# Other scratch for one input product, and the bonus product of the second half beside the key norm's transposes

## The chip, the cores and the metric

The kernel runs on one core of one Trainium2 chip. The metric is the device time of one execution in microseconds (us). TensorE (PE in the profile) does the matmuls and the transposes, PEld is its weight load, DVE is VectorE, ACT is ScalarE, POOL is GpSimd, SP issues most of the weight transfers.

## The reference

One block in float32: a gated feed-forward network with half weight, a hybrid mixer, and a second feed-forward network, each between two root-mean-square norms, for 256 tokens of width 2048. The change lies in the mixer's recurrent branch (RWKV-7, width 1024, 16 heads of 64):

```python
r, k, v, lw, la, lg = jnp.split(zs, RWKV_SPLITS, axis=-1)      # zs = z + (shifted z - z) * mu
w = -jax.nn.softplus(-(w0 + jnp.tanh(lw) @ w2)) - 0.5
decay = jnp.exp(-jnp.exp(w))
a = jax.nn.sigmoid(a0 + la @ a2)
g = jax.nn.sigmoid(lg) @ g2
kk = k * k_k, divided by its norm in each head
k = k * (1.0 + (a - 1.0) * k_a)
y = _wkv7_scan(r_h, decay, k_h, v_h, -kk, kk * a_h)            # the recurrence over 256 tokens
y = group norm of y, * gn_w + gn_b
bonus = jnp.sum(r_h * k_h * r_k, axis=-1, keepdims=True) * v_h
y = (y + bonus) * g
```

r, k and v are columns of `p = u @ w_in`. The bonus needs r, the new k and v, and nothing of the recurrence.

## The kernel before, in words

All large products are made in three matmuls of 128x128 by 128x512 each, from operands split into a high and a low part (lines 367, 368 and 369). A weight tile of 128x1024 comes by a transfer on SP (line 329, buffers `w32`, four of them), is cast by ScalarE into its high part (line 343) and subtracted by VectorE into its low part (line 344); five buffers of each part stand between them and TensorE.

The mixer computes the recurrent branch in two halves of 512 columns (8 heads). For each half, three input products give k, v and r (`z_g`, through `across`). Such a product ends with these steps, which need three scratch tiles, here `sg`, `T1` and `x32`: ScalarE copies the result from PSUM to `sg` (line 1136), VectorE transposes blocks of 32 from `sg` to `T1` (line 1138), GpSimd issues 16 transfers from `T1` to `x32` (line 1147), and `shift` mixes each column with the one before, into the tile `zk`, `zv` or `zr` (ScalarE at line 1588, VectorE at line 1591).

`scratch` gives those three tiles. For products of the first half it hands out three of the 15 tiles R0 to R14 in turn; for the second half, three tiles of the pool `up`. That pool has `NUNITS = 33` places of 128x1024; a tile takes a place when it is first written and gives it back after its last reader. The 15 tiles R, the split input (8 tiles), results and `zk`, `zv`, `zr` all live in it.

`rwkv` is the recurrent branch of one half, written as a generator; the same R tiles serve both halves. Its steps in order, with their lines:

- kk = k * k_k (1845) to R3, its square (1846) to R5; small products pn (1852) for the head norms; pw and pa (1838, 1839) for decay and `a`; the sigmoids of the decay to R0 (1862) and of `a` to R2 (1869); running sums (1875) to R4; the exponentials `lam` to R0 (1879) and `ilam` to R1 (1880).
- transposes of v into the state (pV, 1905, copied out at 1910 and 1911).
- transposes of the norms (pk, 1919); kk times pk (1925).
- k2, the new k, to R5: ScalarE at 1927, VectorE at 1929, which is the last reader of `zk`; the products with `lam` and `ilam` (1930 to 1943), into R7 to R12.
- qb = r * r_k * k2 to R6 (1947), on VectorE.
- transposes and scores (pB 1963, pA 1976), with their masks (1985, 1987).
- the bonus: qb summed over each head by a product with a block of ones (pb, 2003), times v (2004).
- an inversion by substitution in 31 steps on VectorE (2020, 2022), and then the recurrence in four chunks.

Three things set the order of the work. TensorE's order is written by hand in the mixer (`manual_schedule`): `weave` runs `rwkv` to its next `yield x` and then puts x us of other products (`rest`: the remaining input products, the gates `gb_g`, `pb_g`) between. The order on the other engines is the planner's, which takes what is ready by priority, earlier program text first; weight casts and the ends of products have raised priority. PSUM has four banks (`pt`) for all the small products here and four for the large ones.

The first half's products, in order, are the low-rank inputs, two of the pooling branch, k, v and r. So they are the first to sixth call of `scratch`.

Of the kernel before, what the change touches and what calls it, by code (L numbers as in the profile page):

```python
# [12 lines left out]
AF = mybir.ActivationFunctionType  # L13
ALU = mybir.AluOpType
# [5 lines left out]
S = 256  # L20
# [241 lines left out]
class Block:  # L262
# [1330 lines left out]
    def mixer(s, prm, uT, rs, resid, emit, gpost, reload):  # L1593
# [49 lines left out]
        z = [{}, {}]  # L1643

        def z_g(hf, part=0):
            for nme, zc in ((("k", 1), ("v", 2), ("r", 0)), (("k", 1),),
                            (("v", 2), ("r", 0)), (("v", 2),), (("r", 0),))[part]:
                z[hf][nme] = s.unit((P, 4, S), F32, "z" + nme)
                c0 = zc * W + hf * 512
                yield from s.across(w_in, c0, at, rs, lambda v: s.shift(  # L1650
                    v, c0 // P, [z[hf][nme][:, i] for i in range(4)]), scratch(hf))
# [25 lines left out]
        turn = itertools.count()  # L1677

        def scratch(hf=0):
            n = next(turn)  # L1680
            if hf:
                return [s.unit(p="sc") for _ in range(3)]
            return [s.R[(3 * n + i) % 15] for i in range(3)]

        def pool_g(b):
            def done(v):
# [119 lines left out]
    def rwkv(s, hf, z, lz, prm, yH, yL):  # L1806
        nc = s.nc
        V, A, G, T = nc.vector, nc.scalar, nc.gpsimd, nc.tensor
        col = lambda nme, i: s.col[nme][:, hf * 4 + i:hf * 4 + i + 1]
# [4 lines left out]
        def reg(n, *shape):  # L1814
            t = s.R[n]
            if len(shape) == 2:
                return t.rearrange("p (a b) -> p a b", a=shape[0])
            if len(shape) == 3:
                return t.rearrange("p (a b c) -> p a b c", a=shape[0], b=shape[1])
            if len(shape) == 4:  # L1820
                return t.rearrange("p (a b c d) -> p a b c d", a=shape[0], b=shape[1],
                                   c=shape[2])
            return t
        ch = lambda t: t.rearrange("p i (c t) -> p i c t", c=NCH)
        fl = lambda t: t.rearrange("p i t -> p (i t)")
# [14 lines left out]
        k, v = z["k"], z["v"]  # L1840
# [17 lines left out]
        for q in range(2):  # L1858
            ps = s.psum("pw").rearrange("p (i t) -> p i t", i=2)
            lora(ps, 0, q)  # L1860
            for i in range(2):
                A.activation(out=sw[:, 2 * q + i], in_=ps[:, i], func=AF.Sigmoid,
                             bias=col("w0", 2 * q + i))
        a = reg(2, 4, S)
        for q in range(2):
            ps = s.psum("pa").rearrange("p (i t) -> p i t", i=2)
            lora(ps, 1, q)
            for i in range(2):
                A.activation(out=a[:, 2 * q + i], in_=ps[:, i], func=AF.Sigmoid,
                             bias=col("a0", 2 * q + i))  # L1870
# [29 lines left out]
        for pr in range(2):  # L1900
            pss = []
            for src in (v, vs):
                ps = s.psum("pV").rearrange("p (i c) -> p i c", i=4)
                for i in range(4):
                    T.transpose(ps[:, i], src[:, i, pr * P:pr * P + P], s.ident)
                pss.append(ps)
            for b in range(2):
                c = 2 * pr + b
                pe, po = pss[1 - b], pss[b]
                A.copy(EVs[O, :, c], pe[O, :, :64])  # L1910
                A.copy(ODs[E, :, c], po[E, :, 64:])
        yield 8.5
        pks = []
        for q in range(2):
# [3 lines left out]
                    o = h * 512 + (2 * q + i) * P  # L1918
                    T.transpose(ps[:, i, h * P:h * P + P], nbf[:, o:o + P], s.ident)
            pks.append(ps)  # L1920
        r = z["r"]
        k2 = reg(5, 4, S)
        for q in range(2):
            i2 = slice(2 * q, 2 * q + 2)
            V.tensor_tensor(out=kk[:, i2], in0=kk[:, i2], in1=pks[q], op=ALU.mult)
            for i in (2 * q, 2 * q + 1):
                A.activation(out=k2[:, i], in_=a[:, i], func=AF.Identity, scale=col("k_a", i),
                             bias=col("oka", i))
            V.tensor_tensor(out=fl(k2[:, i2]), in0=fl(k2[:, i2]), in1=fl(k[:, i2]), op=ALU.mult)
            V.tensor_tensor(out=fl(a[:, i2]), in0=fl(kk[:, i2]), in1=fl(a[:, i2]), op=ALU.mult)  # L1930
            for h, R in ((0, E), (1, O)):
                g8 = lambda t, sl: t[R, :, :, sl].rearrange("p i c t -> p (i c) t")
                V.tensor_tensor(out=g8(BK[q], h), in0=gr(a[R, i2]), in1=gr(ilam[R, i2]),
                                op=ALU.mult)
                V.tensor_tensor(out=g8(BK[q], 1 - h), in0=gr(k2[R, i2]), in1=gr(ilam[R, i2]),
                                op=ALU.mult)
                aa = g8(AR[q][h], 0)
                V.scalar_tensor_tensor(out=aa[:, :, 1:], in0=gr(kk[R, i2])[:, :, 1:],
                                       scalar=-1.0, in1=gr(lam[R, i2])[:, :, :C - 1],
                                       op0=ALU.mult, op1=ALU.mult)  # L1940
                V.tensor_scalar(out=aa[:, :, :1], in0=gr(kk[R, i2])[:, :, :1], scalar1=-1.0,
                                scalar2=None, op0=ALU.mult)
                V.tensor_tensor(out=g8(AR[q][h], 1), in0=gr(r[R, i2]), in1=gr(lam[R, i2]),
                                op=ALU.mult)
        qb = reg(6, 4, S)
        for i in range(4):
            V.scalar_tensor_tensor(out=qb[:, i], in0=r[:, i], scalar=col("r_k", i),
                                   in1=k2[:, i], op0=ALU.mult, op1=ALU.mult)
        lc = s.small(16, "lc", bufs=1)
        V.tensor_copy(lc, gr(lam)[:, :, C - 1])  # L1950
        lc4 = lc.rearrange("p (i c) -> p i c", i=4)
# [43 lines left out]
        yield 5.5  # L1995
        scores(1, 0)
        scores(1, 1)
        yield 6

        for q in range(2):  # L2000
            pb = s.psum("pb").rearrange("p (i t) -> p i t", i=2)
            for i in range(2):
                T.matmul(pb[:, i], s.bones, qb[:, 2 * q + i], start=True, stop=True)
            V.tensor_tensor(out=qb[:, 2 * q:2 * q + 2], in0=pb, in1=v[:, 2 * q:2 * q + 2],
                            op=ALU.mult)
        G.memset(EVs[E, :, 0], 0.0)
        G.memset(ODs[O, :, 0], 0.0)

# [8 lines left out]
        for kq in range(31):  # L2017
            n, m = kq // 2 + 1, 31 - kq
            pr = s.rtmp("pr")[:, :n * m].rearrange("p (a b) -> p a b", a=n)
            V.tensor_tensor(out=pr, in0=wt[:, kq + 1:, kq].unsqueeze(1).to_broadcast([P, n, m]),  # L2020
                            in1=tw[:, :n, kq:kq + 1].to_broadcast([P, n, m]), op=ALU.mult)
            V.tensor_tensor(out=tw[:, :n, kq + 1:], in0=tw[:, :n, kq + 1:], in1=pr,
                            op=ALU.add)
# [9 lines left out]
            A.copy(tt[R, :, o:o + 32], td[R])  # L2033
        for h in range(2):
            G.memset(tt[h * 64 + 32:h * 64 + 64, :, :32], 0.0)
        yield 44
        ps = s.psum("pM").rearrange("p (g t) -> p g t", g=16)
        for g in range(16):
            for h in range(2):
# [7 lines left out]
        for g in range(16):  # L2047
            for h in range(2):
                R = slice(h * 64 + 32, h * 64 + 64)
                T.matmul(ps[h * 64:h * 64 + 32, g], m1[R, g], tt[R, g, 32:64],  # L2050
                         start=True, stop=True)
# [13 lines left out]
        for c in range(NCH):  # L2065
            yield 1.8 if c else 0
            pu = v4(s.psum("pU"))
            for i in range(4):
                for R, h, ev in ((E, 0, EVs), (O, 1, ODs)):
                    T.matmul(pu[R, i], AR[i // 2][h][:, i % 2, c, 0], ev[:, i, c],  # L2070
                             start=True, stop=True)
# [14 lines left out]
            if c < NCH - 1:  # L2086
                pS = v4(s.psum("pS"))
                for i in range(4):
                    for R, h in ((E, 0), (O, 1)):
                        T.matmul(pS[R, i], BKt[i // 2][:, i % 2, c, h], ea_[:, h, i],  # L2090
                                 start=True, stop=True)
                st = s.rtmp("st").rearrange("p (i t) -> p i t", i=4)
                for R, ev in ((E, EVs), (O, ODs)):
                    V.tensor_tensor(out=st[R], in0=pS[R], in1=ev[R, :, c], op=ALU.add)
                    V.tensor_tensor(out=ev[R, :, c + 1], in0=st[R],
                                    in1=lc4[R, :, c:c + 1].to_broadcast([64, 4, C]),
                                    op=ALU.mult)
            py = v4(s.psum("pY"))
            for i in range(4):
                for R, h, ev in ((E, 0, EVs), (O, 1, ODs)):  # L2100
                    T.matmul(py[R, i], AR[i // 2][h][:, i % 2, c, 1], ev[:, i, c],
                             start=i == 0, stop=False, skip_group_check=True)
            for i in range(4):
                for R, h in ((E, 0), (O, 1)):
                    T.matmul(py[R, i], Xrb[R, i * NCH + c], ea_[R, h, i],  # L2105
                             start=False, stop=i == 3, skip_group_check=True)
# [5 lines left out]
                            op=ALU.subtract)  # L2112
# [5 lines left out]
                            op0=ALU.mult, op1=ALU.add)  # L2118
# [3 lines left out]
                            op=ALU.mult)  # L2122
# [11 lines left out]
        for q in range(2):  # L2134
# [7 lines left out]
            for i in range(2):  # L2142
                ii = 2 * q + i
                V.scalar_tensor_tensor(out=qb[:, ii], in0=pt[:, i], scalar=col("gn_w", ii),
                                       in1=qb[:, ii], op0=ALU.mult, op1=ALU.add)
                V.scalar_tensor_tensor(out=qb[:, ii], in0=qb[:, ii], scalar=col("gn_b", ii),
                                       in1=pg[:, i], op0=ALU.add, op1=ALU.mult)
            A.copy(yH[:, 2 * q:2 * q + 2], qb[:, 2 * q:2 * q + 2])
            V.tensor_tensor(out=yL[:, 2 * q:2 * q + 2], in0=qb[:, 2 * q:2 * q + 2],
                            in1=yH[:, 2 * q:2 * q + 2].bitcast(F32), op=ALU.subtract)  # L2150
# [108 lines left out]
```

## Time and profile before

| | |
|---|---|
| time, median of 3 runs (lowest to highest) | 2000.14 us (1999.96 to 2001.76) |
| the profiled execution | 2002.03 us |
| its span, first to last instruction | 2000.3 us |
| mean granted TensorE clock | 0.998 |
| busy: PE, DVE, ACT, POOL | 1987.1, 1812.9, 1223.4, 410.0 us |
| transferred | 472.37 MB, mean 236 GB/s |

The mixer with its recurrent branch lies between about 650 and 1330 us of the span. Times of instructions below are counted from the start of the span. In a list of instructions in order of time the columns are start, duration of the (possibly merged) row, engine, line, operation, tiles as out<-in, shapes, count, and in brackets the idle time of that engine just before and what ended it. A row for a stretch gives the busy time and the count of each engine, then the granted clock of TensorE, the share of the transfer engines, and GB/s.

### The profile page before, as it was taken

To read this page: it belongs to the slowest core of one execution; us is meant where nothing else is said; L and a number is where in the kernel's file an instruction comes from. 1 tells how busy PE (TensorE), PEld (TensorE's weight loads), DVE (VectorE), ACT (ScalarE), POOL (GpSimd) and SP (SyncE) were. 2 spreads that over 40 slices of the span, in tenths; PEclk is the share of its full clock that TensorE was granted. 3 is DMA by queue.
4 is the path that set the end of the run, shared out by engine and by line. 5 is a ranking of instruction groups with operands and counts; after the bars stand their busy time and mean duration, and the time that the engine had idled before them with its cause. 6 is when DMAs were issued, how large, how long until landed. Compare 5 with 4: busy or idle time off the path is not lost.

```text
span 2000.3 us, 29053 instructions
## 1 busy us (share of the span) xinstructions
PE 1987.1 (99%) x9903; PEld 1645.3 (82%) x9903; DVE 1812.9 (91%) x2467; ACT 1223.4 (61%) x1631; POOL 410.0 (20%) x747
## 2 busy tenths in 40 slices
PE   9999999999999999999999999999999999999998
PEld 7888888888888888888788888888888888888886
DVE  7999999999999957789789678989999999999997
ACT  7566665666666566675566434675666666666653
POOL 2000000574100113412320112010000115650000
PEclk9999999999999999999999999999999999999999
DMA  9868896987877777757556648869688889887774
GB/s 346 268 209 268 249 261 226 275 265 234 231 227 254 270 202 213 199 179 214 154 163 186 179 159 257 303 221 296 219 250 265 245 271 267 266 264 227 234 261 169
DMA packets 254086, 472.37 MB, mean 236 GB/s; under 512 B 27379, under 2 KB 31088, under 8 KB 253936
## 3 DMA queue, kind: packets, MB, share of 16 engines
q1 hardware_dynamic: 214128, 400.89, 61.0%
q0 software_dynamic: 39520, 69.08, 15.3%
q8 instruction: 78, 1.28, 0.3%
q14 instruction: 72, 0.59, 0.1%
q10 hardware_dynamic: 288, 0.52, 0.1%
HBM read 445.45 MB, written 8.39 MB: 227 GB/s over the span
## 4 chain that ended last, share of the span: by engine, by line
PE 97%; DVE 1%; issue 1%; ACT 1%; DMA 1%; SPq 0%; POOLq 0%; POOL 0%; DVEq 0%; ACTq 0%
PE mm L367 26%; PE mm L369 25%; PE mm L368 25%; PE ms L368 6%; PE ms L369 6%; PE ms L367 6%; PE tr L1015 1%; PE pA L1976 0%; DMA w<-in_w_in_dram 0%; DMA w<-in_ffn_gate_dram 0%; PE mc L977 0%; PE pU L2070 0%; PE pSa L2082 0%; PE pY L2105 0%; PE pT L2140 0%
## 5 line engine op out<-in xcount | busy, mean ns | idle before, releaser
L367 PE MATMUL mm<-wH,xH 128*128 128x512 f32 (+1 forms) x2008 | 783.2, 390 | 0.2 <-ACT xH L1024 0.2
L368 PE MATMUL mm<-wL,xH 128*128 128x512 f32 (+1 forms) x2008 | 779.3, 388 | 0.0
L369 PE MATMUL mm<-wH,xL 128*128 128x512 f32 (+1 forms) x2008 | 779.2, 388 | 0.1
L369 PEld LDWEIGHTS mm<-wH,xL 128*128 128x128 f32 x2008 | 377.2, 188 | 78.6 <-DVE xL L1033 1.1
L367 PEld LDWEIGHTS mm<-wH,xH 128*128 128x128 f32 x2008 | 377.1, 188 | 78.3 <-ACT xH L1024 0.5
L368 PEld LDWEIGHTS mm<-wL,xH 128*128 128x128 f32 x2008 | 377.2, 188 | 75.7 <-DVE wL L431 0.2
L677 ACT CAST wH<-t 128x1024 fp32r<-128x1024 f32 x244 | 256.8, 1054 | 209.5 <-DVE t L669 96.0
L421 ACT CAST wH<-w 128x1024 fp32r<-128x1024 f32 x293 | 301.6, 1052 | 118.7 <-PE mm L369 100.2
L431 DVE TENSOR_TENSOR wL<-w,wH 128x1024 fp32r<-128x1024 f32 x293 | 350.5, 1218 | 18.4 <-ACT wH L421 16.6
L343 ACT CAST wH<-w 128x1024 fp32r<-128x1024 f32 (+2 forms) x184 | 188.4, 1029 | 180.1 <-PE mm L369 155.4
L344 DVE TENSOR_TENSOR wL<-w,wH 128x1024 fp32r<-128x1024 f32 (+2 forms) x184 | 217.5, 1189 | 88.0 <-ACT wH L343 86.5
L682 DVE TENSOR_TENSOR wL<-t,wH 128x1024 fp32r<-128x1024 f32 x244 | 293.1, 1217 | 3.2 <-ACT wH L677 2.3
L677 ACT CAST wH<-w 128x1024 fp32r<-128x1024 f32 x244 | 199.6, 836 | 120.9 <-PE mm L369 91.0
L682 DVE TENSOR_TENSOR wL<-w,wH 128x1024 fp32r<-128x1024 f32 x244 | 229.1, 951 | 0.3
L1058 POOL DMA_DIRECT2D x<-T x352 | 179.0, 560 | 145.9 <-DVE wL L682 46.7
L655 POOL DMA_DIRECT2D t<-in_ffn_up_dram x47 | 57.4, 1227 | 567.3 <-DMA t<-in_ffn_up_dram 178.4
L368 PE MATMUL ms<-wL,sH 128*128 128x512 f32 x312 | 121.4, 389 | 0.0
L367 PE MATMUL ms<-wH,sH 128*128 128x512 f32 x312 | 121.4, 389 | 0.0
L369 PE MATMUL ms<-wH,sL 128*128 128x512 f32 x312 | 121.4, 389 | 0.0
L669 DVE TENSOR_TENSOR t<-w,t 128x512 f32<-128x512 f32 x122 | 83.4, 684 | 0.4 <-DMA w<-in_ffn_down_dram 0.2
L665 DVE TENSOR_TENSOR t<-w,t 128x512 f32<-128x512 f32 x122 | 82.9, 684 | 0.1
L660 DVE TENSOR_TENSOR t<-w,w 128x1024 f32<-128x1024 f32 x60 | 73.0, 1218 | 3.3 <-DMA w<-in_ffn_down_dram 3.3
(354 smaller groups left out, 2309.8 us busy)
## 6 DMA issues: line engine op xcount, KB each, us to landing
w<-in_w_in_dram SPq DMA_DIRECT2D x128, 512.0 KB, 4.4
w<-in_ffn_down_dram SPq DMA_DIRECT2D x104, 512.0 KB, 6.1
w<-in_ffn_up_dram SPq DMA_DIRECT2D x94, 512.0 KB, 5.7
w<-in_ffn_gate_dram SPq DMA_DIRECT2D x92, 512.0 KB, 6.9
w<-in_ffn_gate_dram SPq DMA_DIRECT2D x168, 256.0 KB, 5.8
w<-in_ffn_down_dram SPq DMA_DIRECT2D x131, 256.0 KB, 4.8
w<-in_ffn_up_dram SPq DMA_DIRECT2D x117, 256.0 KB, 5.9
t<-in_ffn_up_dram POOLq DMA_DIRECT2D x47, 512.0 KB, 7.7
```

The source lines that it names most:

```text
L343: s.nc.scalar.copy(vH, v)
L344: s.nc.vector.tensor_tensor(out=vL, in0=v, in1=vH.bitcast(F32), op=ALU.subtract)
L367: nc.tensor.matmul(ps, aH, bH, start=start, stop=False, skip_group_check=seeded)
L368: nc.tensor.matmul(ps, aH, bL, start=False, stop=False, skip_group_check=seeded)
L369: nc.tensor.matmul(ps, aL, bH, start=False, stop=stop, skip_group_check=seeded)
L421: nc.scalar.copy(x["H"], x["v"])
L431: nc.vector.tensor_tensor(out=x["L"], in0=x["v"], in1=x["H"].bitcast(F32), op=ALU.subtract)
L665: V.tensor_tensor(out=v["t24"][:, 0], in0=v["a"][:, 0], in1=v["t13"][:, 1], op=ALU.add)
L669: V.tensor_tensor(out=v["t24"][:, 1], in0=v["b"][:, 1], in1=v["t24"][:, 0], op=ALU.add)
L677: nc.scalar.copy(H, src)
L682: V.tensor_tensor(out=L, in0=src, in1=H.bitcast(F32), op=ALU.subtract)
L1058: nc.gpsimd.dma_start(out=x[0][q * 32:q * 32 + 32, i], in_=src[i * 32:i * 32 + 32, q])
```

## The change

`scratch` takes the start of the three R tiles from a list: the sixth call, r of the first half, now gets R6 to R8 instead of R0 to R2. The second half does not count its calls any more and takes tiles of the pool as before.

In `rwkv`, the work on k2, the weighing and the bonus become three local functions. In the first half they stand where they stood. In the second half, k2 (`extra`) and the weighing (`weigh`) stand ahead of the 8.5 us of filling before pk, and the bonus stands directly behind the transposes pk. The 6 us of filling that stood ahead of the bonus are added to the 44 us before the next product.

```diff
         def scratch(hf=0):
-            n = next(turn)
             if hf:
                 return [s.unit(p="sc") for _ in range(3)]
-            return [s.R[(3 * n + i) % 15] for i in range(3)]
+            n = (0, 3, 6, 9, 12, 6)[next(turn)]
+            return s.R[n:n + 3]
...
                 A.copy(ODs[E, :, c], po[E, :, 64:])
+        r = z["r"]
+        k2 = reg(5, 4, S)
+        qb = reg(6, 4, S)
+
+        def extra(q):
+            for i in (2 * q, 2 * q + 1):
+                A.activation(out=k2[:, i], in_=a[:, i], func=AF.Identity, scale=col("k_a", i),
+                             bias=col("oka", i))
+            V.tensor_tensor(out=fl(k2[:, 2 * q:2 * q + 2]), in0=fl(k2[:, 2 * q:2 * q + 2]), in1=fl(k[:, 2 * q:2 * q + 2]), op=ALU.mult)
+
+        def weigh():
+            for i in range(4):
+                V.scalar_tensor_tensor(out=qb[:, i], in0=r[:, i], scalar=col("r_k", i),
+                                       in1=k2[:, i], op0=ALU.mult, op1=ALU.mult)
+
+        def bonus():
+            for q in range(2):
+                pb = s.psum("pb").rearrange("p (i t) -> p i t", i=2)
+                for i in range(2):
+                    T.matmul(pb[:, i], s.bones, qb[:, 2 * q + i], start=True, stop=True)
+                V.tensor_tensor(out=qb[:, 2 * q:2 * q + 2], in0=pb, in1=v[:, 2 * q:2 * q + 2],
+                                op=ALU.mult)
+        if hf:
+            extra(0)
+            extra(1)
+            weigh()
         yield 8.5
         pks = []
...
-        r = z["r"]
-        k2 = reg(5, 4, S)
+        if hf:
+            bonus()
         for q in range(2):
             i2 = slice(2 * q, 2 * q + 2)
             V.tensor_tensor(out=kk[:, i2], in0=kk[:, i2], in1=pks[q], op=ALU.mult)
-            (k2 on ScalarE and VectorE)
+            if not hf:
+                extra(q)
...
-        (qb = r * r_k * k2)
+        if not hf:
+            weigh()
...
         scores(1, 1)
-        yield 6
-        (pb and its product with v)
+        if not hf:
+            yield 6
+
+        if not hf:
+            bonus()
...
-        yield 44
+        yield 50 if hf else 44
```

More of the change, by code (lines that the diff above doesn't have):

```diff
@@ L1925, in rwkv @@
             V.tensor_tensor(out=kk[:, i2], in0=kk[:, i2], in1=pks[q], op=ALU.mult)
[L1926 to L1929, printed above, removed]
+            if not hf:
+                extra(q)
             V.tensor_tensor(out=fl(a[:, i2]), in0=fl(kk[:, i2]), in1=fl(a[:, i2]), op=ALU.mult)
@@ L1944, in rwkv @@
                                 op=ALU.mult)
[L1945 to L1948, printed above, removed]
+        if not hf:
+            weigh()
         lc = s.small(16, "lc", bufs=1)
@@ L1997, in rwkv @@
         scores(1, 1)
-        yield 6
[L2000 to L2005, printed above, removed]
+        if not hf:
+            yield 6
+        if not hf:
+            bonus()
         G.memset(EVs[E, :, 0], 0.0)
```

## The prediction

> **What bounds the kernel now.** I read the totals and the chain of work first, then the busy time by stretches, then the orders of TensorE, ScalarE, VectorE and GpSimd around the two edits.
>
> ```profile
> span 2000.3 us, 29053 instructions
> PE 1987.1 (99%) x9903; PEld 1645.3 (82%) x9903; DVE 1812.9 (91%) x2467; ACT 1223.4 (61%) x1631; POOL 410.0 (20%) x747
> ...
> PE 97%; DVE 1%; issue 1%; ACT 1%; DMA 1%; SPq 0%; POOLq 0%; POOL 0%; DVEq 0%; ACTq 0%
> ```
>
> TensorE holds 97% of the chain. The order of its queue is written by hand, so what the change can give or take is time in which TensorE stands still; work on other engines is free as long as TensorE does not wait for it. The stretches of the mixer show where it stands:
>
> ```profile
> core 0: us, PE busy (x) PEld busy (x) DVE busy (x) ACT busy (x) POOL busy (x), PEclk, DMA share, GB/s
> 850.00:900.00 50.00, 48.48 (x285) 40.35 (x284) 43.68 (x74) 37.70 (x69) 8.02 (x9) 1.00 0.59 179
> 1000.00:1050.00 50.00, 50.00 (x337) 42.62 (x336) 41.65 (x76) 32.99 (x50) 12.91 (x20) 1.00 0.55 162
> ```
>
> The first half of the recurrence (around 850 us) loses 1.52 us; the start of the second half (1000 to 1050 us) loses nothing. So the first edit aims at a real hole, and the second touches a place that has none.
>
> **First edit: the scratch of r in the first half.** Before, r's product uses R0 to R2, and `a` (L1869) is written to R2, so `a` stands behind the last reading of r's scratch (L1588). `a` holds two of the four small PSUM banks meanwhile. TensorE and ScalarE there:
>
> ```profile
> 855.17 0.60 PE L1905 MATMUL pV<-ident,zv 128*128 128x128 f32 x4
> 855.61 0.60 PE L1905 MATMUL pV<-ident,R 128*128 128x128 f32 x4
> 857.73 0.66 PE L1905 MATMUL pV<-ident,zv 128*128 128x128 f32 x4 [1.52 <-ACT R L1910]
> 858.38 0.66 PE L1905 MATMUL pV<-ident,R 128*128 128x128 f32 x4
> 858.79 0.47 PE L367 MATMUL mm<-wH,xH 128*128 128x512 f32 x1
> ```
> ```profile
> 848.52 1.57 ACT L1862 ACTIVATE R<-pw,cols 128x256 f32<-128x256 f32 x4 [0.93 <-PE pw L1839]
> 864.25 0.91 ACT L1588 ACTIVATE zb<-R,cols 128x256 f32<-128x256 f32 x2
> 866.31 1.28 ACT L1869 ACT_TABLE_LOAD   x1
> 867.61 1.57 ACT L1869 ACTIVATE R<-pa,cols 128x256 f32<-128x256 f32 x4
> ```
>
> The four groups of pV want four banks. The banks of pn and pw are free (L1862 ended at 850.1), but both of pa are held until 869, so the third group waits until the first two are copied out. Four groups at 0.44 us (855.17 to 855.61) are 1.76 us; they took 855.17 to 858.79, 3.62. With R6 to R8 as scratch, `a` needs only pa and follows L1862 directly, until about 851.7, well ahead of 855. R6 to R8 become qb and BK later; their earlier user is a pool product two products back, so I price the new claim at nothing. Also gone is the table load at 866.31 (sigmoid before the exponential, not after): ScalarE time, off the path. Term: **-1.9 us** (bounds 0 and -1.9). What is late next is the weights: some casts already wait for their transfers a little later,
>
> ```profile
> 885.25 1.05 ACT L343 CAST wH<-w 128x1024 fp32r<-128x1024 f32 x1 [1.97 <-DMA w<-in_w_in_dram]
> 888.22 1.05 ACT L343 CAST wH<-w 128x1024 fp32r<-128x1024 f32 x1 [1.92 <-DMA w<-in_w_proj_b_dram]
> ```
>
> and a TensorE that arrives 1.9 us sooner could give some of it back there; but TensorE has no wait in that stretch now, and the work on ScalarE and VectorE that crowds 860 to 876 moves earlier too. I keep -1.9 and let 0 stand as the other end.
>
> **Second edit: the bonus beside pk.** Moved ahead of pk in the second half: four activations and two products (k2, `extra`), four weighings (`weigh`); moved from 6 us of filling after the scores to directly behind pk: four matmuls and two VectorE products (`bonus`). No DMA is issued by them, and the filling of TensorE is the same (44+6 became 50). What they cost themselves:
>
> ```profile
> 1038.33 1.04 PE L1919 MATMUL pk<-ident,R 128*128 128x128 f32 x8
> 1039.12 0.47 PE L367 MATMUL mm<-wH,xH 128*128 128x512 f32 x1
> ...
> 1082.51 1.89 PE L2003 MATMUL pb<-R,bones 128*128 128x256 f32 x8
> 1084.04 0.58 PE L367 MATMUL mm<-wH,xH 128*128 128x512 f32 x1
> ```
>
> pb takes 1.53 us (1082.51 to 1084.04) in either place. One change between small and large matmuls goes: a first L367 of 0.58 instead of 0.39, **-0.1 us** at most -0.2. Two VectorE products of 0.6 us leave the long series behind the scores, which hides them.
>
> The point is what pb waits for. `weigh` reads r, so pb now needs r of the second half when pk is done, at 1039.1. Before, when is that r ready?
>
> ```profile
> 976.31 0.69 ACT L1136 ACTIVATE sc<-mm,rs 128x512 f32<-128x512 f32 x1 [1.84 <-PE mm L369]
> ...
> 1031.92 0.69 DVE L1929 TENSOR_TENSOR R<-R,zk 128x512 f32<-128x512 f32 x1
> 1032.53 1.22 DVE L344 TENSOR_TENSOR wL<-w,wH 128x1024 fp32r<-128x1024 f32 x1
> 1033.66 1.30 DVE L1138 STREAM_TRANSPOSE sc<-sc 128x512 f32<-128x512 f32 x2
> ...
> 1062.47 0.48 DVE L1947 SCALAR_TENSOR_TENSOR R<-zr,cols,R 128x256 f32<-128x256 f32 x1
> ```
>
> r leaves PSUM at 977, but its transposes come only at 1033.66, and the last weighing ends at 1062.95. The code says why: `s.unit` has 33 places, claimed at the first write. At 977 there are live 15 R, 8 of the input, lq, 2 of the finished first yT, 4 yb, zk, zv and the copy just made: 33. The transposes need one more, and the next to fall free is zk, whose last reader is the second L1929. It is the instruction just before them but for one weight product. The change does not free a place: L1929 is in `extra`, behind the same `a`. After the transposes comes GpSimd:
>
> ```profile
> 1035.25 6.46 POOL L1147 DMA_DIRECT2D sc<-sc x13 [6.28 <-DVE sc L1138]
> 1042.45 0.98 POOL L1147 DMA_DIRECT2D sc<-sc x2 [0.74 <-DMA sc<-sc]
> 1044.09 0.50 POOL L1147 DMA_DIRECT2D sc<-sc x1 [0.66 <-DMA sc<-sc]
> DMA to landing us min/median/max: 2.5/4.5/6.4
> ```
>
> Sixteen copies fill every part of r's transposed form, so nothing of r can be shifted before the last has landed. It is issued at 1044.09; by 2.5 to 6.4 us it lands between 1046.6 and 1050.5. I take 3.5, between the least and the median, because GpSimd had waited for earlier copies to land and few are before it: 1047.6. Then the shift and the weighing:
>
> ```profile
> 1053.43 0.51 ACT L1588 ACTIVATE zb<-sc,cols 128x256 f32<-128x256 f32 x1
> 1053.84 0.50 ACT L1588 ACTIVATE zr<-sc,omu 128x256 f32<-128x256 f32 x1
> 1054.71 0.89 DVE L1591 TENSOR_TENSOR zr<-zr,zb 128x256 f32<-128x256 f32 x2
> ```
>
> Eight activations at 0.41 (1053.43 to 1053.84) are 3.3 us, one sum 0.45, one weighing 0.48: 4.2, with 0.1 for the hand-overs 4.3, so the last operand stands at 1051.9. ScalarE and VectorE are free for it, for with TensorE standing no weight buffer falls free and no cast is due. The last half of pb is 0.8 more: filling goes on at 1052.7. Without the wait it would at 1039.12 + 1.53 = 1040.65. Term: **+12.0 us** of standing TensorE, which nothing covers, since every matmul is queued behind pb.
>
> Bounds: at the short end L1929 comes as early as its input allows.
>
> ```profile
> 1024.88 1.14 ACT L1927 ACTIVATE R<-R,oka,cols 128x256 f32<-128x256 f32 x2
> ...
> 1030.17 1.09 ACT L1927 ACTIVATE R<-R,oka,cols 128x256 f32<-128x256 f32 x2
> ```
>
> If the second pair followed the first, before the exponentials, all behind it would be 4.1 us earlier (1030.17 to 1026.0), and with the least landing another 1.0: +6.9. At the long end the shift keeps its old date, last weighing 1062.95 plus 0.8: +23.1. I am nearest to the middle, because the exponentials stand ahead of k2 in the program in both kernels, and because the casts that delayed L1588 before are not there when TensorE stands.
>
> **The clock.** A standing TensorE also comes back slow. This run has one such place, its start, after an idle of 1.33 us:
>
> ```profile
> 6.86 0.66 PE L1015 MATMUL tr<-ident,x 128*128 128x128 f32 x4 [1.33 <-DMA x<-in_x_dram]
> ```
> ```profile
> 8.00:10.00 2.00, 1.74 (x4) 0.63 (x4) 1.90 (x7) 2.00 (x7) 1.58 (x4) 0.67 1.07 397
> 10.00:12.00 2.00, 2.00 (x8) 1.71 (x8) 1.56 (x4) 0.90 (x4) 0.41 (x1) 0.50 1.05 385
> 12.00:14.00 2.00, 2.00 (x10) 1.64 (x9) 1.50 (x5) 1.40 (x3) 0.00 (x0) 0.98 1.05 372
> ```
>
> Granted 0.67, 0.50 and 0.98: 0.66 + 1.00 + 0.04 = 1.7 us of clock lost. But the 1.52 us hole at 856 left the clock at 1.00, so idle does not always cost. For 11 us of idle I take the start's value: **+1.7 us** (bounds 0 and 1.7). The Trainium skill, page "TensorE: Matmul & The Clock Gate", Part 1, speaks against the change: after an idle window of about 3.4 us the clock drops to half and needs about 3.4 us of activity to return. By that page alone the hole at 856 is too short to count, as the trace has it, and the new one would cost an estimated 1.7 us; the start's drop after 1.33 us is not what its window leads one to expect.
>
> **Sum.** -1.9 - 0.1 + 12.0 + 1.7 = +11.7 us. The profiled execution took 2002.0 us with a span of 2000.3; it stands 1.9 above the median of 2000.14. A span of 2012.0, and against the median 2011.8, which I give as **2011.8**.
>
> **Rivals.** (1) Short wait: L1929 and the copies move up, +6.9 instead of +12.0, giving 2006.7, or 2005.0 without the clock's term. For it: VectorE no longer has L1935 ahead of the second L1929 in the program. Against: the exponentials come first, and GpSimd's sixteen issues keep their 9.3 us. (2) Long wait: shift late, +23.1, 2022.9; for it the old date of L1588, against it the empty ScalarE. (3) No wait, the other side: r's transposes get a place before the second half starts, so that r is weighed before pk is done. All r's steps from L1138 on take 1033.66 to 1051.9, 18.2 us, so this decides from a place free by 1020.9; then only -1.9 - 0.1 is left, 1998.1. Against it is the count of 33; for it, that 56 us pass between 977 and 1033 and one freed place would do. (4) The first edit brings nothing, because the weights are late at 885: 2013.7, inside the forecast's own range.
>
> **How the numbers follow.** Forecast with rival 4, 0.60, own range 2008 to 2016; short wait 0.20, 2003 to 2008; long wait 0.09, 2016 to 2023; no wait 0.11, around 1998. Leaving out most of no wait and the upper part of the long one gives 2003 to 2018. About 0.2% (4.0 us) is what a measurement of this kernel can tell from no change. No wait lies within that, save 0.03 for a larger gain in the first half; a tenth of the short waits ends below 2004.1: faster 0.03, same 0.10, slower 0.87.
>
> **What would show it.** First half: no idle before the third pV group, L1869 right behind L1862, and no table load before it. Second half: one idle of TensorE of some 9 to 12 us at pb, directly behind pk, released by VectorE's weighing (the first half of pb may run 2 us sooner); L1138 still right behind the second L1929; L1588 within a microsecond of the last landing; a granted clock near 0.5 for the 3 us after it. The prediction is wrong if r's transposes stand well ahead of 1033, if TensorE goes from pk to pb without a hole, or if the filling after it finds weights missing.

## The result, and the profile after

| | before | after |
|---|---|---|
| median (lowest to highest) | 2001.08 us (1999.96 to 2003.08), 5 runs | 2018.89 us (2016.32 to 2022.57), 5 runs |
| ratio after/before, 95% interval | | 1.009, 1.0079 to 1.0101 |
| the profiled execution, its span | 2002.03, 2000.3 us | 2016.32, 2014.6 us |
| mean granted clock of the profiled execution | 0.998 | 0.995 |

The change makes the kernel slower by 17.8 us. The forecast was 11.7; the median lies 0.9 us above the end of the range (2018.0). The profiled execution of the changed kernel is the fastest of its five, so the profile shows less than the medians do.

The page of the changed kernel, span, busy time and chain:

```profile
span 2014.6 us, 29018 instructions
...
PE 1988.2 (99%) x9903; PEld 1645.3 (82%) x9903; DVE 1814.0 (90%) x2467; ACT 1224.4 (61%) x1631; POOL 408.3 (20%) x747
...
PE 95%; DVE 2%; ACT 1%; issue 1%; DMA 1%; POOL 0%; POOLq 0%; DVEq 0%; SPq 0%; ACTq 0%
```

Hardly anybody's work grew (TensorE 1988.2 against 1987.1 us), yet the span did: TensorE stands still more. Its share of the chain fell from 97% to 95%, and VectorE's rose from 1% to 2%. The stretches of the changed kernel say where:

```profile
core 0: us, PE busy (x) PEld busy (x) DVE busy (x) ACT busy (x) POOL busy (x), PEclk, DMA share, GB/s
850.00:900.00 50.00, 48.10 (x284) 40.11 (x283) 42.76 (x68) 36.92 (x68) 6.10 (x8) 1.00 0.59 176
1000.00:1050.00 50.00, 39.12 (x272) 33.56 (x273) 40.87 (x78) 31.87 (x54) 12.92 (x20) 0.92 0.55 158
1050.00:1100.00 50.00, 48.11 (x274) 38.95 (x274) 31.94 (x46) 27.97 (x50) 2.68 (x5) 0.94 0.48 137
```

The stretch from 1000 us stood full before; now 10.9 us of it are empty. The first half (from 850 us) still loses 1.90 us, where it lost 1.52. TensorE's own rows, in order of time:

```profile
854.16 0.60 PE L1905 MATMUL pV<-ident,R 128*128 128x128 f32 x4
854.60 0.60 PE L1905 MATMUL pV<-ident,zv 128*128 128x128 f32 x4
...
878.60 0.50 PE L368 MATMUL mm<-wL,xH 128*128 128x512 f32 x1 [1.90 <-DVE wL L344]
...
1036.83 1.04 PE L1945 MATMUL pk<-ident,R 128*128 128x128 f32 x8
1048.75 2.05 PE L1931 MATMUL pb<-R,bones 128*128 128x256 f32 x4 [10.88 <-DVE R L1924]
1052.68 2.04 PE L1931 MATMUL pb<-R,bones 128*128 128x256 f32 x4 [1.89 <-DVE R L1924]
1054.17 0.99 PE L367 MATMUL mm<-wH,xH 128*128 128x512 f32 x1
```

The hole ahead of the third pV group is gone, and a new one of 1.90 us stands 24 us later, at a large product that waits for the low part of a weight. In the second half TensorE waits 10.88 and 1.89 us between pk and the end of pb.

Numbering the large products and setting the start of each beside that of the same product before gives the steps of the difference: -1.96 us at pV, +2.06 at 878.60, -0.29 near 965, +16.55 at the product behind pb (1039.12 before, 1054.17 here), +0.87 over the next three, -1.73 at 1084, where pb used to be. With the steps too small to list this is +15.7. The span differs by only 14.3, because the start-up of this execution was shorter: from 13 us on every product stands 1.41 us earlier than before. That has nothing to do with the change. The granted clock stayed at 1.00 from 8 to 14 us here, where it had fallen to 0.50 before.

ScalarE, VectorE and GpSimd of the changed kernel around both edits:

```profile
847.01 1.57 ACT L1862 ACTIVATE R<-pw,cols 128x256 f32<-128x256 f32 x4 [0.86 <-PE pw L1839]
848.46 0.86 ACT L1869 ACTIVATE R<-pa,cols 128x256 f32<-128x256 f32 x2
...
1046.71 0.51 ACT L1588 ACTIVATE zb<-sc,cols 128x256 f32<-128x256 f32 x1 [10.00 <-DMA sc<-sc]
```
```profile
1030.44 0.69 DVE L1920 TENSOR_TENSOR R<-R,zk 128x512 f32<-128x512 f32 x1
1031.04 1.22 DVE L344 TENSOR_TENSOR wL<-w,wH 128x1024 fp32r<-128x1024 f32 x1
1032.17 1.30 DVE L1138 STREAM_TRANSPOSE sc<-sc 128x512 f32<-128x512 f32 x2
...
1049.38 1.38 DVE L1967 TENSOR_TENSOR R<-zr,R 64x512 f32<-64x512 f32 x2
1050.79 0.76 DVE L1591 TENSOR_TENSOR zr<-zr,zb 128x256 f32<-128x256 f32 x2
1051.46 0.68 DVE L1932 TENSOR_TENSOR R<-pb,zv 128x512 f32<-128x512 f32 x1
1052.06 0.87 DVE L1924 SCALAR_TENSOR_TENSOR R<-zr,cols,R 128x256 f32<-128x256 f32 x2
```
```profile
1033.76 6.49 POOL L1147 DMA_DIRECT2D sc<-sc  x13 [6.29 <-DVE sc L1138]
...
1043.65 0.50 POOL L1147 DMA_DIRECT2D sc<-sc  x1 [1.62 <-DMA sc<-sc]
```

The chain of the stall is read from the bottom up: the last of r's sixteen copies is issued at 1043.65, the shift (L1588) starts at 1046.71 after ScalarE has stood for 10.00 us, and the last weighing ends at 1052.93. L1138, the first step of that chain, stands two instructions behind the second k2 product (L1920), the last reader of `zk`.

### The profile page after: what moved, and what is told of

The parts are those of the page before. It is cut to its first block, busy times and chain, and to the rows that moved or that the text cites. A ratio compares the mean times of both kernels' runs of the same rounds, so it can differ in the third digit from the quotient of the medians.

```text
span 2014.6 us, 29018 instructions
## 1 busy us (share of the span) xinstructions
PE 1988.2 (99%) x9903; PEld 1645.3 (82%) x9903; DVE 1814.0 (90%) x2467; ACT 1224.4 (61%) x1631; POOL 408.3 (20%) x747
## 4 chain that ended last, share of the span: by engine, by line
PE 95%; DVE 2%; ACT 1%; issue 1%; DMA 1%; POOL 0%; POOLq 0%; DVEq 0%; SPq 0%; ACTq 0%
PE mm L367 25%; PE mm L369 25%; PE mm L368 25%; PE ms L369 5%; PE ms L367 5%; PE ms L368 5%; PE tr L1015 1%; DMA sc<-sc 0%; PE pA L1998 0%; ACT wH L343 0%; DVE wL L344 0%; PE pU L2089 0%; PE pSa L2101 0%; DMA w<-in_ffn_gate_dram 0%; PE pY L2124 0%
```

## The experiments

The kernels ran in three groups, each beside 21 runs of the kernel before.

| kernel | median (lowest to highest), runs | ratio, 95% interval |
|---|---|---|
| before, first group | 2000.67 (1999.93 to 2002.91), 21 | |
| e1_scratch | 2002.98 (2001.11 to 2004.11), 11 | 1.0009, 1.0000 to 1.0018 |
| e2_bonus | 2016.60 (2015.70 to 2017.73), 4 | 1.008, 1.0066 to 1.0093 |
| e3_place | 2004.26 (2001.79 to 2005.06), 11 | 1.0016, 1.0007 to 1.0025 |
| e5_filled | 2017.92 (2015.04 to 2021.96), 4 | 1.0087, 1.0074 to 1.0101 |
| before, second group | 2000.63 (1999.54 to 2002.44), 21 | |
| e6_filled2 | 2016.73 (2014.86 to 2017.45), 5 | 1.0077, 1.0065 to 1.009 |
| e7_k2_early | 2000.25 (1999.74 to 2003.42), 11 | 1.0, 0.9991 to 1.0009 |
| e8_place_only | 2001.46 (2000.71 to 2002.25), 11 | 1.0002, 0.9994 to 1.0011 |
| e9_mix_apart | 2017.13 (2016.52 to 2018.93), 4 | 1.0082, 1.0069 to 1.0096 |
| before, third group | 2000.50 (1999.79 to 2003.01), 21 | |
| e10_weigh_late | 2003.65 (2001.78 to 2004.51), 11 | 1.0014, 1.0005 to 1.0023 |
| e13_late_alone | 2001.15 (2000.38 to 2001.78), 11 | 1.0, 0.9991 to 1.0009 |
| e12_weigh_first | 2018.78 (2017.31 to 2019.19), 5 | 1.0089, 1.0076 to 1.0103 |

**The two edits apart.** e1_scratch is the kernel before with the first edit alone:

```diff
         def scratch(hf=0):
-            n = next(turn)
             if hf:
                 return [s.unit(p="sc") for _ in range(3)]
-            return [s.R[(3 * n + i) % 15] for i in range(3)]
+            n = (0, 3, 6, 9, 12, 6)[next(turn)]
+            return s.R[n:n + 3]
```

> The first edit alone. Theory W (the 1.96 us that the third pV group no longer waits are given back 25 us later, where TensorE waits for a weight's low part behind VectorE's queue, 1.90 us in the changed kernel): the same time as before, within 0.5 us of it, no idle before the third pV group and one of 1.5 to 2 us at about 879 us. Rival F (the give-back comes from the second edit's new order on VectorE, not from the first edit): 1.9 us faster than before, no idle at 879.

Measured: 2.3 us above the kernel before, at the edge of what can be told from no change, and no gain; the idle ahead of the third pV group is gone and one of 1.90 us stands at 879, as expected. The time was expected within 0.5 us of before. TensorE and its stretches in e1_scratch:

```profile
879.66 0.50 PE L368 MATMUL mm<-wL,xH 128*128 128x512 f32 x1 [1.90 <-DVE wL L344]
```
```profile
880.00:882.00 2.00, 2.00 (x8) 1.58 (x7) 2.00 (x4) 0.87 (x2) 0.00 (x0) 0.67 0.61 143
882.00:884.00 2.00, 2.00 (x6) 1.62 (x5) 1.97 (x4) 0.75 (x1) 0.00 (x0) 0.50 0.80 224
884.00:886.00 2.00, 2.00 (x10) 1.55 (x10) 1.97 (x4) 0.72 (x2) 0.00 (x0) 0.97 0.83 246
```

The 1.96 us won at pV are lost again 23 us later in one wait of 1.90 us. In this execution the granted clock falls behind that wait to 0.67, 0.50 and 0.97: 0.66 + 1.00 + 0.06 = 1.7 us, most of the 2.3 by which the medians differ. In the profiled execution of the changed kernel the same wait left the clock at 1.00.

Which weight product is late shows when casts and low parts are counted, in order of time. ScalarE's casts and VectorE's low parts in e1_scratch, then the same two rows in the kernel before:

```profile
870.59 1.05 ACT L343 CAST wH<-w 128x1024 fp32r<-128x1024 f32 x1
```
```profile
866.59 1.22 DVE L344 TENSOR_TENSOR wL<-w,wH 128x1024 fp32r<-128x1024 f32 x1
...
872.03 1.21 DVE L344 TENSOR_TENSOR wL<-w,wH 128x1024 fp32r<-128x1024 f32 x1
...
878.39 1.22 DVE L344 TENSOR_TENSOR wL<-w,wH 128x1024 fp32r<-128x1024 f32 x1
```
```profile
873.11 2.00 ACT L343 CAST wH<-w 128x1024 fp32r<-128x1024 f32 x2
```
```profile
867.08 1.23 DVE L344 TENSOR_TENSOR wL<-w,wH 128x1024 fp32r<-128x1024 f32 x1
...
870.20 1.21 DVE L344 TENSOR_TENSOR wL<-w,wH 128x1024 fp32r<-128x1024 f32 x1
...
876.90 1.22 DVE L344 TENSOR_TENSOR wL<-w,wH 128x1024 fp32r<-128x1024 f32 x1
```

In e1_scratch the third wide cast behind 865 us ends at 871.6, but its low part stands on VectorE only at 878.39; before, the same cast ended at 874.1 and its low part started at 876.90. So the cast came 2.5 us sooner and its low part 1.5 us later: VectorE's order now has more of the recurrent products ahead of it, which the earlier `a` had made ready. The delay arises one low part earlier: from the first to the second row of e1_scratch 5.44 us pass, before only 3.12, because two products of k2 and `ilam` (L1935), two sums of r's shift (L1591) and one weighing (L1947) now stand in between. There was little room for it. Before, this low part ended at 878.12 and TensorE used it at 879.94, so its slack was 1.8 us.

e2_bonus is the second edit alone (the diff of the change without the hunk above).

> The second edit alone. Theory R (TensorE stands at pb until r of the second half is weighed, and the clock comes back late): 17 to 18 us slower than before, all of what the whole change costs, with the idle of 1.5 us at the third pV group back and no idle at 879. Rival S (the two edits act on each other, so that the first one's new order makes r later in the second half): less than 14 us slower.

Measured: +15.9 us on the median, and by its trace a step of 15.88 us at the product behind pb, with another 2.0 us at half clock right behind it. There is no idle at 879. It was expected to cost 17 to 18 us, and one sign failed: the idle of 1.52 us at the third pV group did not come back whole, but is 0.40 us. It is as short in the other kernels without the first edit (0.66 in e7_k2_early, 0.49 in e8_place_only, 0.40 in e13_late_alone), with ScalarE in the same order there. In the profile of the kernel before, two of ScalarE's casts ahead of pV's copies waited 0.82 and 0.72 us for weight transfers; in these four only one waits, 0.34 to 0.78 us. So the size of that hole hangs on the execution. Together with e1_scratch, 2.3 + 15.9 = 18.2 us, which is what the whole change costs against the same 2000.67: as far as spreads of 2 to 6 us can tell, the edits add up.

**Is it the place in the pool?** e3_place is the changed kernel, in which r's transposed form and its copy in the second half lie in R8 and R4, which are free by then, and not in pool places:

```diff
             if hf:
+                if len(z[1]) == 3:
+                    return [s.unit(p="sc"), s.R[8], s.R[4]]
                 return [s.unit(p="sc") for _ in range(3)]
```

> The changed kernel, with the second and third scratch tile of the second half's r in R8 and R4 (which the first half no longer needs then) instead of two places of the pool. Theory R (r's transposes wait for zk's place in the pool): they run at about 977 instead of 1032, r is ready by 1005, TensorE passes from pk to pb without an idle, and the time is that of before within 1 us. Rival G (GpSimd's sixteen issues and their transfers set when r is ready, wherever the tiles lie, because GpSimd serves the recurrence then): the idle at pb stays over 8 us and the time at least 10 us above before. Rival C (r is early, but the sixteen issues now delay GpSimd's copies for the recurrence): no idle at pb, but 2 to 6 us lost between 977 and 1000.

Measured: 14.6 us less than the changed kernel's median. TensorE, ScalarE and GpSimd in e3_place:

```profile
1000.65 0.68 PE L2103 MATMUL pSa<-us,R 64*64 64x64 f32 x16 [1.11 <-ACT us L2098]
...
1041.08 1.04 PE L1947 MATMUL pk<-ident,R 128*128 128x128 f32 x8
1041.95 1.89 PE L1933 MATMUL pb<-R,bones 128*128 128x256 f32 x8
```
```profile
997.32 0.50 ACT L1588 ACTIVATE zb<-R,cols 128x256 f32<-128x256 f32 x1
...
1000.24 0.36 ACT L2098 COPY us<-pU 128x256 f32<-128x256 f32 x1
```
```profile
979.91 5.38 POOL L1147 DMA_DIRECT2D R<-R  x11 [2.50 <-DVE g L2130]
```

The copies are issued from 979.91 instead of 1033.76, the shift starts at 997.32 instead of 1046.71, and pb runs behind pk without a hole. So without r's wait for a place there is no stall, and GpSimd's sixteen copies alone don't make one. The time was expected within 1 us of the kernel before and is 3.6 us above it. The sooner shift costs 1.19 us elsewhere: its activations and a copy (L1900) occupy ScalarE while the recurrence of the first half waits for a copy (L2098), and TensorE stands for 1.11 us. The rest is about what e1_scratch shows for the first edit (2.3 us): here, too, a wait of 1.90 us stands at 879 and the clock falls behind it.

e8_place_only has the same places on e2_bonus, without the first edit.

> The second edit alone, with the second half's r in R8 and R4, and the first half's scratch as before. Theory R+C (the place takes away the whole wait at pb; GpSimd's sixteen issues in the recurrence cost the 1.2 us seen at 998; the 2.4 us more of the version with both edits came from the first edit's weights and clock): 2000 to 2002, within 0.1% of before, no idle at pb. Rival W2 (the loss at 880 us belongs to the second edit's order of VectorE too): 2003 to 2005 as with both edits.

Measured: no difference from the kernel before. Its trace has -1.03 us at pV (the shorter hole that e2_bonus has too), +1.20 us at 998, pb moved (+1.61, -1.53), and no idle at pb.

e7_k2_early moves k2 and the weighing of the second half ahead, and leaves pb where it was:

```diff
+        if hf:
+            extra(0)
+            extra(1)
+            weigh()
         yield 8.5
...
         (pb and its product stay behind the scores, `yield 6` and `yield 44` in both halves)
```

> The kernel before with k2 and the weighing of the second half put ahead of pk as in the change, and pb left in its old place behind the scores; no other scratch. Theory R (only the place of pb costs, since r is weighed by 1065 us at the latest): the time of before within 1 us, no idle at pk or pb, and only up to 1.1 us gained or lost at the first half's pV from the planner's new order. Rival V (k2 and the weighing, moved ahead on VectorE, delay the weights or the scores): 3 us or more above before with an idle between 1040 and 1080.

Measured: no difference. That r is late costs nothing as long as no matmul stands behind it. The stall needs both: r late, which e3_place and e8_place_only take away, and pb early, which this kernel takes away.

**What of the stall is the clock?** e5_filled puts 24 products of the ones with a constant, read by nobody, ahead of the first pb of the second half, so that TensorE stays busy over the long wait; e6_filled2 also puts 6 ahead of the second pb. The diff is that of e6_filled2; e5_filled has 0 in place of the 6:

```diff
                 pb = s.psum("pb").rearrange("p (i t) -> p i t", i=2)
+                for _ in range((24, 6)[q] * hf):
+                    T.matmul(pb[:, 0], s.bones, s.rsb, start=True, stop=True)
```

> The changed kernel with 24 further products of the block of ones by a constant ahead of the first pb, into the same bank, which the first pb then overwrites: 10.4 us of TensorE work inside its idle of 10.9 us. The wait for r is as long as before; only the clock is kept up. Theory K (the clock costs the 2 us that the profile shows, in pb and the first products behind it, and the rest of what the runs above the profiled one take): 2.5 to 4 us faster than the changed kernel, 2015 to 2016.5, and the five runs lie within 2 us of each other instead of 6. Rival N (the clock costs nothing that matters, the runs vary by transfers): the time of the changed kernel, 2018 to 2019, with the same spread.

> The changed kernel with 24 further products ahead of the first two matmuls of pb and 6 ahead of the last two, so that both waits of TensorE for r are filled with work (the last wait, 2.48 us with the 24 alone, was followed by 3.4 us at half clock). Theory K (the clock falls even behind a wait of 2 to 2.5 us, and that is what the 24 alone could not take away): the granted clock stays at 1.00 through 1036 to 1060 us, the first large product behind pb comes 1.5 to 2 us sooner after pk than the 16.55 us more of the changed kernel, and the median is 2015 to 2016.5. Rival N (what is lost beyond the wait is not the clock's): clock 1.00 and still 2017.5 to 2019.

TensorE and two stretches of e5_filled, then of e6_filled2:

```profile
1054.53 1.83 PE L1933 MATMUL pb<-R,bones 128*128 128x256 f32 x4 [2.48 <-DVE R L1924]
```
```profile
1054.00:1056.00 2.00, 1.47 (x5) 1.24 (x5) 1.99 (x4) 0.00 (x0) 0.00 (x0) 0.69 0.00 0
1056.00:1058.00 2.00, 2.00 (x6) 1.54 (x6) 0.76 (x2) 0.19 (x1) 0.00 (x0) 0.50 0.00 0
```
```profile
1053.43 1.08 PE L1933 MATMUL pb<-R,bones 128*128 128x256 f32 x4
```
```profile
1054.00:1056.00 2.00, 2.00 (x11) 1.66 (x10) 1.70 (x3) 0.26 (x2) 0.00 (x0) 1.00 0.00 0
```

In e5_filled the long wait is filled, but the second one of 2.48 us is left, and the clock falls behind it all the same, so the filling brings nothing that can be told (2017.92 against 2018.89, with both spreads over 6 us). The wait at 879 had lowered the clock in this execution too (0.67, 0.50, 0.98 from 880 to 886 us), so it is no clean test. In e6_filled2 the clock stays at 1.00; the median is 2.2 us below the changed kernel's, and the runs lie within 2.6 us instead of 6.3, though the two ranges overlap. Its rows say it more closely: the last weighing ends as long after the start of pk as in the changed kernel (16.1 us), the step at pb is 15.73 instead of 16.55, and the +0.87 behind it is gone. That is 1.7 us for the clock; the rest is waiting. Theory K had the clock right and its effect on the step too large (0.8 us, where 1.5 to 2 were expected). As the fillers ended only at 1053.4, 0.3 us before the last weighing, they cost at most little themselves.

**Can the first edit's gain be kept?** e9_mix_apart changes TensorE's order on top of e1_scratch: the input product of k goes ahead of the last pooling product.

```diff
-            yield from s.seq([gb_g(1), mix_g(2), mix_g(3), z_g(1, 1), pb_g(0), ...
+            yield from s.seq([gb_g(1), mix_g(2), z_g(1, 1), mix_g(3), pb_g(0), ...
```

> The first edit alone, and the two pooling products of the filling (mix_g 2 and 3, short products of TensorE whose weights take two of the four load buffers) set apart by the second half's k. Theory W (the gain at pV is real and is lost only where the weights are short behind these two): no idle at 879, the 1.96 us are kept, 1998 to 1999.5, a version faster than both kernels. Rival X (the shortage moves with TensorE and comes at another place): 2000.5 to 2003.

Neither theory foresaw what came. The wait at 879 shrank from 1.90 to 0.55 us, and a new one appeared, in TensorE's and ScalarE's rows:

```profile
922.37 0.80 PE L367 MATMUL mm<-wH,yb 128*128 128x512 f32 x1 [13.34 <-ACT yb L1798]
```
```profile
917.77 0.51 ACT L1588 ACTIVATE zb<-sc,cols 128x256 f32<-128x256 f32 x1 [7.66 <-DMA sc<-sc]
...
921.85 0.47 ACT L1798 ACTIVATE yb<-mc,cols 128x256 fp32r<-128x256 f32 x1
```

The copy-out of the pooling product (L1798) stands on ScalarE behind the shift of k, and that behind GpSimd's copies: the same chain as r's, hit at another place. Whether L1798 waited in ScalarE's order alone or also for a pool place isn't told apart. As a test of the weights it is inconclusive.

e10_weigh_late is e1_scratch with the first half's weighing put behind the scores in the program, ahead of pb; e13_late_alone is that move without the first edit. In both, the weighing of the first half reads R5 after the scores have been written there, so the first half's bonus is made of other numbers by the same instructions.

```diff
         qb = reg(6, 4, S)
-        (four weighings)
+        if hf:
+            weigh()
...
+        if not hf:
+            weigh()
         for q in range(2):
             pb = s.psum("pb").rearrange("p (i t) -> p i t", i=2)
```

> The kernel before with the first edit, and in the first half the four weighings of r (1.9 us of VectorE) stand behind the scores in the program. Theory V (the first edit's gain is lost because VectorE is full from 862 to 886, and the k2, kk and weighing that now come sooner stand ahead of a weight's low part, line 344): that low part comes 1 to 1.9 us sooner, TensorE's wait at 879 shrinks from 1.90 to under 1 us, the clock does not fall there, time 1999 to 2001.5. Theory W (the weight's transfer is late, whatever VectorE has to do): the wait stays at 1.9 us and the time at 2003.

> The kernel before with the weighing of the first half behind the scores alone, without the first edit. Both theories: no wait at 879 before and none now, 2000.6 within 1.5 us. It is the base against which the first edit is read in the run with both.

TensorE and VectorE in e10_weigh_late:

```profile
880.26 0.50 PE L368 MATMUL mm<-wL,xH 128*128 128x512 f32 x1 [2.25 <-DVE wL L344]
```
```profile
878.59 0.48 DVE L1799 SCALAR_TENSOR_TENSOR yb<-mc,cols,yb 128x256 fp32r<-128x256 f32 x1
878.99 1.22 DVE L344 TENSOR_TENSOR wL<-w,wH 128x1024 fp32r<-128x1024 f32 x1
```

The wait grew to 2.25 us, and e13_late_alone is the kernel before. Theory V falls as it was put: with 1.9 us less ahead of it on VectorE the low part came no sooner; other work, an L1799 among it, took the room. Its rival came nearer in its numbers (wait 1.9, time 2003; measured 2.25 and 2003.65), but falls in its cause, for the cast shows the weight to have been there: it had ended at 871.9. What remains is VectorE's fixed order itself, in which the planner has put that low part behind the recurrent products; no kernel that moves it alone was tried.

**Some of the stall VectorE's order?** e12_weigh_first is the changed kernel with the weighing of the second half at the raised priority:

```diff
-            weigh()
+            with s.tc.high_priority(offset=BOOST):
+                weigh()
```

> The changed kernel with the second half's weighings at the raised priority that the weight products have. Theory O (some 2 us of the wait at pb are VectorE's order, two products with r and one with pb put ahead of the last weighings): the last weighing ends about 1.4 to 2 us sooner against the last landing, and the step at pb is 14 to 15 us instead of 16.5, time 2016.5 to 2017.5. Theory L (all of the wait is the way of r, landing, shift and sums): the step stays at 16.5, time 2018 to 2019.

Measured: the changed kernel's time, and a step of 16.72 us at pb. But VectorE's order didn't change; in e12_weigh_first the two products with r (here L1968) and pb's product still stand ahead of the last two weighings:

```profile
1050.07 1.38 DVE L1968 TENSOR_TENSOR R<-zr,R 64x512 f32<-64x512 f32 x2
...
1052.16 0.68 DVE L1932 TENSOR_TENSOR R<-pb,zv 128x512 f32<-128x512 f32 x1
1052.76 0.87 DVE L1924 SCALAR_TENSOR_TENSOR R<-zr,cols,R 128x256 f32<-128x256 f32 x2
```

So this run doesn't decide between the two theories, though its time is that of theory L; the share of VectorE's order is read from rows, not shown.

## Why the prediction was right and wrong

**Right: the mechanism and its place.** One stall between pk and pb, released by the weighing; L1138 still right behind the second k2 product; r's lateness a matter of pool places. e3_place and e8_place_only show that there is no stall without the wait for a place, and e7_k2_early that there is none without pb's new position. The rival "no wait" falls, as does "long wait": the shift started with the last landing and not at its old date of 1053.43. "Short wait" falls too: k2 came no sooner than forecast.

**Wrong: the first edit's -1.9 us.** The hole at pV went, L1869 follows L1862, and no table load stands ahead of it, all as said. But the step "I keep -1.9" failed, and outside its bounds of 0 and -1.9. Rival 4, by which the edit brings nothing, was nearer, for a reason that was half named. TensorE, 1.96 us sooner, met a low part that was 1.5 us later than before. The forecast looked for the weights at 885, at their transfers; the miss came at 879, on VectorE, at a weight whose cast was done 6.8 us earlier. The remark that the work crowding 860 to 876 "moves earlier too" was taken for a help; by VectorE's rows it was what stood ahead of the low part, which no kernel tested alone. By e1_scratch the edit costs 2.3 us, not -1.9: in its trace a step of 2.06 us at the wait takes back the gain of 1.96, and the clock behind it adds about 1.7. This is the largest single error, about 4 us. The size of the gain, too, was read from an execution in which the hole was large: 1.52 us there, 0.40 to 0.66 in the four later profiles without the first edit. The table load didn't go either; it moved, and e1_scratch has it ahead of a gate's sigmoid in the same stretch.

**Mis-sized: the stall, +12.0 us.** Measured, the product behind pb came 16.55 - 1.53 = 15.0 us later than pb alone explains. Against the forecast moved by the 1.5 us by which this execution ran ahead: the last copy was held 1.62 us and not 0.66, and landed within 3.1 us and not 3.5, so that the shift started at 1046.71 and not at 1046.1 (+0.6). From the shift's start to the last weighing 4.3 us were forecast, and it took 6.2 (1046.71 to 1052.93), +1.9: on VectorE the 1.38 us of L1967 and the 0.68 us of L1932 got in between, while the forecast held VectorE free. Behind it the last half of pb and the change to large products ran at half clock, about 0.5 more than the 0.8 forecast for them. The three make 3.0, and 12.0 + 3.0 = 15.0.

**The clock, +1.7.** The effect is there. e6_filled2, which takes it away, is 2.2 us faster on the median and 1.7 us by its rows: 0.8 in the step at pb, which holds the 0.5 above, and 0.9 in the products behind it. Stall and clock together were forecast at 13.7 us and took 15.0 + 0.9 = 15.9. That the 1.7 fits to the tenth is luck, as e2_bonus lost 2.0 us behind pb where this execution lost 0.9. The changed kernel at the end of the stall:

```profile
1054.00:1056.00 2.00, 2.00 (x6) 1.53 (x6) 0.92 (x2) 0.19 (x1) 0.00 (x0) 0.50 0.00 0
1056.00:1058.00 2.00, 2.00 (x11) 1.61 (x10) 0.13 (x1) 1.05 (x1) 0.00 (x0) 1.00 0.02 4
```

The clock was back at full some 2 us after the large products began; both halves of pb, at 1048.75 and 1052.68, had run at half clock.

**The remainder.** The profiled execution shows +15.7 without its start-up, the medians 17.8. e1_scratch lost about 1.7 us of clock behind the 1.90 us wait; the profiled execution of the changed kernel did not. That its other runs did would close most of the 2.1 us. The mean clocks on record point that way: the five runs of the changed kernel go from 2016.32 us at 0.995 to 2022.57 at 0.992, and 0.003 of the span is 6 us, about their whole spread. But no profile of such a run is there, so where they lost it is argued, not shown. Why one wait of 1.90 us lowers the clock and the next doesn't also stays open.

## What to carry to other kernels

Before moving a small product up in a hand-ordered queue, follow each of its operands back to the first resource it needs; here it was a free buffer place, claimed at the first write, that held r for 56 us, with a chain of copies behind it. Take the time from operand ready to operand used from the order that the engine will have, with what becomes ready at the same moment in it, and not from durations on a free engine. And a hole taken out of the critical engine is a gain only if the next operand it meets is early: look at the slack of the following operands on every engine that makes them, not just at the transfers.

## What the runs showed of the hardware

TensorE's granted clock fell to half after idle times much shorter than the long one: after 1.90 us in e1_scratch (0.67, 0.50, 0.97 over 6 us, about 1.7 us lost) and after 2.48 us in e5_filled; the same 1.90 us in the changed kernel left it at 1.00. Of the six profiled executions with this wait of 1.90 us at 879, three lost the clock behind it (e1_scratch, e3_place, e5_filled) and three did not (the changed kernel, e6_filled2, e12_weigh_first). Where it fell, it fell late: a share of 0.67 in the stretch from 880 puts the drop in e1_scratch at about 880.7, an estimate, 1 us after the wait had ended at 879.66.

The Trainium skill, page "TensorE: Matmul & The Clock Gate", Part 1, puts the drop after an idle window of about 3.4 us and the return after about 3.4 us of activity, and calls the window free-running, so that the cold time varies from run to run. The runs here agree in the variation and in the length of the slow time (about 3.4 us in e1_scratch); that 1.90 and 2.48 us suffice differs from the Trainium skill, and the measurement decides.
